# Two of four channel blocks of a depthwise convolution as products with diagonal matrices, and a jump over a loop that is announced

## The chip, the cores and the metric

The kernel runs on one core of a Trainium2 chip. The metric is the device time of one execution in microseconds, as the median of several runs. The engines are PE (TensorE, matrix products), DVE (VectorE), ACT (ScalarE), POOL (GpSimd) and SP (SyncE, whose queue starts the transfers here). Each engine works through its own row of instructions in order and waits on semaphores for the others.

## The reference

All values are float32. A first model (two layers of attention and feed-forward, left out here) gives `x`, 256 tokens of 1024 channels. A second one takes `x` and a context stream of 256 tokens through a mixer "AB" and a mixture of experts, then through a mixer "CD" and another mixture of experts on `x` alone. The change touches two places of it, the convolution of AB and the two mixtures:

```python
def _conv_module(u, conv_w, conv_b, ln_g, ln_b):
    a, gate = jnp.split(u, 2, axis=-1)
    glu = a * jax.nn.sigmoid(gate)
    y = lax.conv_general_dilated(glu, conv_w[:, None, :], window_strides=(1,),
                                 padding=[(CONV_WIDTH // 2, CONV_WIDTH // 2)],
                                 dimension_numbers=('NWC', 'WIO', 'NWC'),
                                 feature_group_count=B_WIDTH) + conv_b
    ...  # layer norm over the channels, then silu

def _mixer_ab(...):
    px = hx @ w_in
    ...
    ox = _dense_attn_blocks(_group(qx, A_KV_HEADS), jnp.concatenate([kc, kx], axis=2), jnp.concatenate([vc, vx], axis=2))
    bx = _conv_module(px[..., o_u:], conv_w, conv_b, ln_g, ln_b)
    yx = jnp.concatenate([_merge(ox), bx], axis=-1) @ w_out

# a mixture: each token goes to 2 of 32 experts
    hid = jax.nn.silu(xb @ w_gate[e]) * (xb @ w_up[e])
    return (hid @ w_down[e]) * wt[:, None]
```

The convolution has 31 taps and 512 channels, each channel on its own: `y[c, t] = sum over j of w[j, c] * glu[c, t + j - 15]`.

## The kernel before

**The convolution.** Channels lie on the partitions, in four blocks of 128; `GT` holds the gated input of a stream with 15 zeros at both ends, `y` (tile `cy`) the sum. For a stream `s` a tap is one instruction on DVE (L1310) over 128 channels and 256 tokens: `y = GT[shifted by j] * w[:, j] + y`; the tap 0 of a block is written by ACT with the bias. So a stream has four first taps on ACT and 120 taps on DVE. They aren't written in one go: `Spare` holds a queue of small pieces of work for an engine, and at each tick of the program (a step of the projections or of the attention of `beside`) an engine is given credit, its `share` of the tick, and takes pieces until the credit is used up. The numbers 0.85 (main stream) and 0.5 (context stream) are those shares. In this way the taps stand in DVE's row between the pieces of the main stream's attention.

**The attention beside it.** A step of the attention makes scores on PE (`acc<-KT,QT`, L1165), the maximum of each row on DVE (L1176, L1178), the exponentials on ACT (`P`, L1183), the transposes of `P` on PE (L788), their copy on ACT (L790) and the product with `V` on PE (L799). Before a head group PE transposes the queries (L1111), and ACT copies them (L1112). In between stand other products of PE (L319 to L321, three for each pair of tiles, with weights that ACT (L300) and DVE (L301) split in two parts). When all taps are done, the sums `cy` are turned by PE (L1339), and the layer norm over channels follows (L1345 to L1362), then the out projection.

**The experts.** `moe` runs over jobs of two experts each; in layer 0 a job "extra" stands at place 8. For a job PE makes gate and up products for the tokens (`project`, L1966, two halves `m` of 16 instructions, which leave 32 records each), ACT and DVE make `hd` of them (L1975, L1983), PE turns `hd` (`hidden_T`, L1989), and the down product follows (L2004). The result of the job before is added to the streams by `combine` for each of the token tiles: PE products with `PT` (L2013, L2065), DVE multiplies by the gate (`tm`, L2023), POOL adds (L2025). The tokens of a job are collected by `match` (DVE, `P`, L1932), `gather` (PE, L2136) and `turn_P` (PE). SP issues the transfers of the weights a fixed number of units ahead, each when a buffer comes free.

**The overflow loop.** Tokens that found no slot in their expert's place are counted in `over`. Behind the job at `i == OVER + 1` (8) all engines load that count (L2232), and if it is 0, as here, they jump over a loop that serves such tokens (L2233). All of the job's combines are written ahead of that jump.

Of the kernel before, what the change touches and what calls it, by code (L numbers as in the profile page):

```python
# [24 lines left out]
NE = 32  # L25
# [5 lines left out]
CONV = ((0.85, 0.1, 4), (0.5, 0.1, 4))  # L31
# [96 lines left out]
def body(tc, d, dump=None):  # L128
    nc = tc.nc
    es = ExitStack()  # L130
    with es:
# [1100 lines left out]
        class MixerAB:  # L1232
            CHUNKS = {"gate": (1280, 512), "a": (768, 512), "kv": (512, 256), "q": (0, 512)}

            def __init__(self, es):
                self.es = es
                wk = self.wk = es.enter_context(tc.tile_pool(name="ab", bufs=1, side="right"))

                for c0, n in ((C_CW, 124), (C_LG, 8)):
                    nc.vector.tensor_scalar(cols[:, c0:c0 + n], cols[:, c0:c0 + n], 0.5, None, op0=OP.mult)  # L1240
                self.tq, self.tk = rope_tables(wk, R_QA, True), rope_tables(wk, R_KA, False)
                self.QT = {1: wk.tile([128, 4, 256], F32, name="QTc")}
                self.KT = wk.tile([128, 512], F32, name="KT")
# [6 lines left out]
                self.spare = Spare(vector=0, gpsimd=0)  # L1250
                on_tick.append(self.beside)
# [52 lines left out]
            def tap(self, s, k, e, j):  # L1304
                w = cols[:, C_CW + 31 * k + j:C_CW + 31 * k + j + 1]
                v, g = self.y[s][:, k], self.GT[s][:, k, j:j + 256]
                if j == 0:
                    nc.scalar.activation(v, g, AF.Identity, scale=w, bias=col(C_CB + k))
                elif e == "vector":
                    nc.vector.scalar_tensor_tensor(v, g, w, v, op0=OP.mult, op1=OP.add)  # L1310
                else:
                    m = self.wk.tile([128, 256], F32, name="tap", bufs=4)
                    nc.scalar.activation(m, g, AF.Copy, scale=w)
                    nc.gpsimd.tensor_tensor(v, v, m, op=OP.add)

            def conv(self, s):
                dve, pool, n = CONV[s]
                self.spare.share = dict(vector=dve, gpsimd=pool)
                for e, ks in (("vector", range(n)), ("gpsimd", range(n, 4))):
                    for j in range(31):  # L1320
                        for k in ks:
                            self.spare.add(e, 0.1 if j == 0 else 0.4 if e == "vector" else 0.7,
                                           lambda k=k, j=j, e=e: self.tap(s, k, e, j))
                    self.spare.add(e, 0.0, lambda: self.half(s))
# [60 lines left out]
            def run(self, sp, norm, norms_done):  # L1385
# [526 lines left out]
        def moe(l, route, u0, during, ending, tail):  # L1912
# [3 lines left out]
            with ExitStack() as ph:  # L1916
# [4 lines left out]
                class Side:  # L1921
# [63 lines left out]
                    def hidden_T(self):  # L1985
# [4 lines left out]
                        self.hT = wr.tile([128, 4, 128], F32, name="hT")[:, :n]  # L1990
                        q3 = q[:, :n * 128].rearrange("p (k s) -> p k s", s=128)
                        nc.scalar.activation(self.hT, q3, AF.Copy)  # L1992
                        self.Y = [wr.tile([128, D], F32R, name="Yh"), wr.tile([128, D], F32R, name="Yl")]

                    def down(self, n, u):

                        if n == 0:
                            self.p = [acc(), acc()]
# [28 lines left out]
                class Half(Side):  # L2027
# [23 lines left out]
                    def down(self, n, u):  # L2051

                        if n == 0:
                            self.p = acc()
# [12 lines left out]
                class Last(Side):  # L2067
# [4 lines left out]
                    def down(self, n, u):  # L2072
                        p = acc()
# [19 lines left out]
                class Late(Half):  # L2093


                    def row(self, e, j, k):
# [14 lines left out]
                class Group:  # L2111


                    def __init__(self, sides, pool=wk):
                        self.sides, self.pool = sides, pool
                        self.n = 256 if pool is wk else 128 * len(sides)
# [22 lines left out]
                    def gather(self, tiles=order):  # L2139
                        XT = self.pool.tile([128, 8, self.n], F32, name="XT")  # L2140
# [27 lines left out]
                extra = []  # L2168
                prev = None
# [12 lines left out]
                for i, j in enumerate(jobs):  # L2182
                    cur = sides.pop(i)
                    if i % 2:

                        sides.update((n, side(jobs[n])) for n in range(i + 1, min(i + 3, len(jobs))))
                        group = Group(list(sides.values())) if sides else None
                        if group:
                            group.match()
                    nxt = sides.get(i + 1)  # L2190
                    for m in range(2):
# [24 lines left out]
                    for n in range(2):  # L2216
                        cur.down(n, u)
                        if nxt and n == 0:
                            nxt.weights()
# [7 lines left out]
                    if i == OVER + 1:  # L2227
                        for t4 in order:
                            prev.combine(t4)
                        prev = None  # L2230

                        total = nc.values_load(route.over[0:1, 0:1], min_val=0, max_val=NT * 4)  # L2232
                        with tc.If(total > 0, preferred_fallthrough_block=False), \  # L2233
                                tc.tile_pool(name=f"ov{l}", bufs=1) as ok:
                            at = ok.tile([128, 1], F32, name="at")
                            nc.vector.memset(at, float(EXTRA[l]))
                            with tc.For_i(0, total):
                                ei, sl, w1 = route.pick(ok, at)
                                e = nc.values_load(ei[0:1, 0:1], engines=(mybir.EngineType.SP,), min_val=0, max_val=NE - 1)
                                s = Late(sl, w1)  # L2240
                                late = Group([s], ok)
                                late.match()
                                late.gather()
                                s.turn_P()
                                s.weights()
                                for m in range(2):
                                    s.act(m, s.project(m, e))
                                s.hidden_T()
                                for n in range(2):
                                    s.down(n, e)  # L2250
                                for t4 in order:
                                    s.combine(t4)
                                nc.vector.tensor_scalar(at, at, 1.0, None, op0=OP.add)
# [289 lines left out]
```

## Time and profile before

| what | value |
| --- | --- |
| median of three runs | 2186.72 us (2186.63 to 2191.0) |
| profiled execution, its own time | 2184.34 us |
| its span | 2182.6 us |
| mean granted clock of PE | 0.964 |
| busy: PE, DVE, ACT, POOL | 91%, 48%, 34%, 18% |
| instructions | 28252 |

The span is what the profile sees of the execution, from the first instruction to the last; the device time has 1.7 us around it. The convolution of the main stream and its attention lie between 859 and 953 us, the experts of layer 0 between 1045 and 1560 us with the jump near 1308 us, those of layer 1 between 1735 and 2182 us with the jump near 1964 us. The shares are means over all stages, and no stage looks like the mean.

### The profile page before, as it was taken

What the parts mean: (1) busy time and instruction counts of PE and PEld (TensorE: products, weight loads), DVE (VectorE), ACT (ScalarE), POOL (GpSimd) and SP (SyncE); (2) the same over time, 40 slices, a digit from 0 to 9 for tenths busy, and PEclk for the clock granted to TensorE, in tenths of its full rate; (3) what the DMA queues carried; (4) which work ended last, traced back from release to release, by engine and by line L of the source; (5) the groups of instructions that cost most, each with busy time, mean ns of one, the idle gap of its engine ahead of it and who ended that gap; (6) DMA issues with size and microseconds to landing.
All of it is one profiled execution on the core that took longest, in us unless ns stands there. A gap on an engine that the chain in (4) does not pass through costs nothing. (4 is left out here: it accounts for less than half of the span.)

```text
span 2182.6 us, 28252 instructions
## 1 busy us (share of the span) xinstructions
PE 1986.8 (91%) x10991; PEld 1262.9 (58%) x10991; DVE 1037.2 (48%) x2123; ACT 734.8 (34%) x1287; POOL 399.3 (18%) x353
## 2 busy tenths in 40 slices
PE   8998999997999988667999998999788799998998
PEld 5765888774898767446444454444366444343343
DVE  5745554664658986957423332333553422222222
ACT  5544544555565456443111110111264311111110
POOL 3000110100110100015132342233420111121111
PEclk8999999999999999788999999999999899999999
DMA  9776777675565443105799997999552699999998
GB/s 324 279 259 211 242 247 267 212 270 176 171 204 174 155 146 115 39 20 203 319 420 414 412 410 295 411 417 417 202 212 78 267 421 421 420 421 383 421 421 340
DMA packets 160765, 612.98 MB, mean 281 GB/s; under 512 B 10528, under 2 KB 16256, under 8 KB 111345
## 3 DMA queue, kind: packets, MB, share of 16 engines
q1 hardware_dynamic: 155744, 596.86, 71.1%
q0 software_dynamic: 4448, 13.51, 2.2%
q8 instruction: 89, 1.46, 0.3%
q10 hardware_dynamic: 432, 0.74, 0.1%
q14 instruction: 52, 0.42, 0.1%
HBM read 607.90 MB, written 3.16 MB: 280 GB/s over the span
## 5 line engine op out<-in xcount | busy, mean ns | idle before, releaser
L1966 PE MATMUL acc<-w,XT 128*64 128x512 f32 x1856 | 435.8, 599 | 19.5 <-DVEq L2233 10.6
L301 DVE TENSOR_TENSOR w<-w 128x1024 fp32r<-128x1024 f32 x244 | 297.9, 1233 | 172.8 <-ACT w L300 154.9
L300 ACT ACTIVATE w<-w 128x1024 fp32r<-128x1024 f32 x252 | 264.5, 1059 | 193.9 <-PE acc L321 92.8
L1966 PEld LDWEIGHTS acc<-w,XT 128*64 128x64 f32 x1856 | 140.1, 138 | 280.8 <-issue 250.9
L2025 POOL TENSOR_TENSOR X<-X,tm 128x512 f32<-128x512 f32 x124 | 155.4, 1281 | 425.1 <-DVE tm L2023 425.1
L2023 DVE TENSOR_TENSOR tm<-acc,gate 128x512 f32<-128x512 f32 x196 | 129.7, 686 | 217.5 <-PE acc L2013 172.1
L2004 PE MATMUL acc<-w,hT 128*64 128x512 f32 x912 | 215.5, 598 | 6.0 <-ACT hT L1992 6.0
L363 PE MATMUL acc<-hi,w 128*128 128x256 f32 x576 | 163.9, 285 | 5.4 <-ACT hi L489 2.2
L364 PE MATMUL acc<-lo,w 128*128 128x256 f32 x576 | 161.9, 281 | 0.8 <-POOL lo L490 0.8
L365 PE MATMUL acc<-hi,w 128*128 128x256 f32 x576 | 161.8, 281 | 0.0
L321 PE MATMUL acc<-w,lo 128*128 128x512 f32 x368 | 150.0, 408 | 1.3 <-POOL lo L1378 1.2
L319 PE MATMUL acc<-w,hi 128*128 128x512 f32 x336 | 142.5, 424 | 6.7 <-ACT hi L1377 5.3
L320 PE MATMUL acc<-w,hi 128*128 128x512 f32 x336 | 137.1, 408 | 8.3 <-DVE w L301 8.2
L1992 ACT ACTIVATE hT<-trp 128x512 f32<-128x512 f32 (+1 forms) x33 | 19.5, 591 | 330.8 <-PE trp L1989 330.8
L1983 DVE SCALAR_TENSOR_TENSOR hd<-sg,ws,acc 128x512 f32<-128x512 f32 (+1 forms) x33 | 36.3, 1099 | 196.5 <-issue 101.0
L2025 POOL TENSOR_TENSOR C<-C,tm 128x512 f32<-128x512 f32 x64 | 79.5, 1272 | 273.8 <-DVE tm L2023 273.8
L2004 PEld LDWEIGHTS acc<-w,hT 128*64 128x64 f32 x912 | 63.4, 136 | 109.6 <-issue 97.4
L363 PEld LDWEIGHTS acc<-hi,w 128*128 128x128 f32 x576 | 108.7, 189 | 8.1 <-ACT hi L489 2.6
L2136 PE MATMUL acc<-P,hi 128*128 128x256 f32 x544 | 104.1, 289 | 8.9 <-issue 6.6
L365 PEld LDWEIGHTS acc<-hi,w 128*128 128x128 f32 x576 | 110.1, 191 | 0.0
L364 PEld LDWEIGHTS acc<-lo,w 128*128 128x128 f32 x576 | 109.1, 189 | 1.5 <-POOL lo L490 1.1
L417 ACT ACTIVATE Yh<-acc 128x512 fp32r<-128x512 f32 x63 | 37.6, 597 | 209.2 <-PE acc L2004 200.2
(423 smaller groups left out, 3427.8 us busy)
## 6 DMA issues: line engine op xcount, KB each, us to landing
w<-in_ex_gate_dram SPq DMA_DIRECT2D x118, 1024.0 KB, 13.2
w<-in_ex_up_dram SPq DMA_DIRECT2D x118, 1024.0 KB, 14.3
w<-in_ex_down_dram SPq DMA_DIRECT2D x118, 1024.0 KB, 13.0
w<-in_ffn_w_dram SPq DMA_DIRECT2D x64, 1024.0 KB, 5.3
fw<-in_mod_w_dram SPq DMA_DIRECT2D x48, 1024.0 KB, 7.5
w<-in_a_w_qkv_dram SPq DMA_DIRECT2D x17, 1024.0 KB, 10.0
w<-in_w_in_ab_dram SPq DMA_DIRECT2D x14, 1024.0 KB, 5.3
w<-in_b_w_qkv_dram SPq DMA_DIRECT2D x12, 1024.0 KB, 5.5
```

What stands on the lines that cost most here:

```text
L300: nc.scalar.activation(wh, w, AF.Copy)
L301: self.engine.tensor_tensor(wl, w, wh.bitcast(F32), op=OP.subtract)
L319: nc.tensor.matmul(ps[:, :n], xh, wh, start=first, stop=False)
L320: nc.tensor.matmul(ps[:, :n], xh, wl, start=False, stop=False)
L321: nc.tensor.matmul(ps[:, :n], xl, wh, start=False, stop=last)
L363: nc.tensor.matmul(z, wh[:, js], xh, start=k == 0 and j % 2 == 0, stop=False)
L364: nc.tensor.matmul(z, wh[:, js], xl, start=False, stop=False)
L365: nc.tensor.matmul(z, wl[:, js], xh, start=False, stop=k == 7 and j % 2 == 1)
L1966: nc.tensor.matmul(p[self.rows(a)], self.XT[:, 4 * k0 + k, self.rows(a)], units[v + a][:, k], start=k0 + k == 0, stop=4 * k0 + k == 7)
L2004: nc.tensor.matmul(self.p[c][self.rows(a)], self.hT[:, 2 * n + k, self.rows(a)], units[v + a][:, k, s], start=n + k == 0, stop=n + k == 2)
L2023: nc.vector.tensor_tensor(g, p, gates[s][:, c], op=OP.mult)
L2025: add.tensor_tensor(dst, dst, g, op=OP.add)
```

## The change

In the main stream's convolution (`CONV[0]`) the blocks 0 and 1 stay as taps on DVE. For the blocks 2 and 3 each tap becomes a product on PE: `sums += diag(w[:, j]) @ GT[shifted by j]`, 62 products that add up in one accumulator over the whole stage (L1341 of the new file, `acc<-GT,dg`), with 62 matrices `dg` that ACT makes by scaling the identity (L1332; four buffers, made three ahead of their use). Two ACT copies with the bias take the sums to `y` at the end. So 60 taps of DVE and two first taps of ACT go. The products are pieces of `Spare` for PE, at 0.43 of credit each and a share of 0.6, from the query projection on. The context stream is as before.

In both mixtures the count and the jump move from behind job `i == 8` into job 9, between `hidden_T` and the down product; the combines of job 8 are all written in the first half of job 9, `match` follows the jump, and `gather` and `turn_P` follow the first part of the down product. The loop's `If` gets a label, a hint for PE names it, and its body is now the block that follows the comparison directly; the block that is taken when nothing is left over stands behind it.

```diff
-CONV = ((0.85, 0.1, 4), (0.5, 0.1, 4))
+CONV = ((0.85, 2), (0.5, 4))
...
+                def weights(i):
+                    if i < len(todo):
+                        diag.append(self.wk.tile([128, 128], F32, name="dg", bufs=4))
+                        nc.scalar.activation(diag[i], ident, AF.Copy, scale=self.weight(*todo[i]))
+
+                def product(i):
+                    if i == 0:
+                        self.sums = acc().rearrange("p (k t) -> p k t", k=2)
+                        for a in range(3):
+                            weights(a)
+                    weights(i + 3)
+                    k, j = todo[i]
+                    nc.tensor.matmul(self.sums[:, k - n], diag[i], self.GT[s][:, k, j:j + 256], start=i == 0, stop=i == len(todo) - 1)
+
+                def end():
+                    for k in range(n, 4):
+                        nc.scalar.activation(self.y[s][:, k], self.sums[:, k - n], AF.Identity, bias=col(C_CB + k))
+                    self.half(s)
+
+                for i in range(len(todo)):
+                    self.spare.add("tensor", 0.43, lambda i=i: product(i))
+                self.spare.add("tensor", 0.0, end)
...
+                    self.spare.share["tensor"] = 0.6
...
+                def left_over():
+
+                    nonlocal ok
+                    total = nc.values_load(route.over[0:1, 0:1], min_val=0, max_val=NT * 4)
+                    with tc.If(total > 0, preferred_fallthrough_block=True, label=f"left{l}"), \
+                            tc.tile_pool(name=f"ov{l}", bufs=1) as ok:
...
+                    loop = i == OVER + 2
+                    if loop:
+                        tc.mark_branch_hint_location(f"left{l}", engines=[mybir.EngineType.PE])
...
-                            for t4 in order[m * half:(m + 1) * half]:
+                            for t4 in order if loop and m == 0 else () if loop else order[m * half:(m + 1) * half]:
                                 prev.combine(t4)
                     cur.hidden_T()
-                    if nxt:
+                    if loop:
+
+                        left_over()
+                        group = next_two()
+                        nxt = sides[i + 1]
+                    elif nxt:
...
-                    if i == OVER + 1:
-                        for t4 in order:
-                            prev.combine(t4)
-                        prev = None
-
-                        total = nc.values_load(route.over[0:1, 0:1], min_val=0, max_val=NT * 4)
-                        with tc.If(total > 0, preferred_fallthrough_block=False), \
-                                tc.tile_pool(name=f"ov{l}", bufs=1) as ok:
```

In PE's row of before, at the start of the main stream's attention (`qr`, `KT`, `QT`, `P`, `PT` and `V` are the queries, keys, probabilities and values), stand:

```order
L1111 MATMUL trp<-cst,qr 128x128 x4
L1165 MATMUL acc<-KT,QT 128x512 x4
L788 MATMUL trp<-cst,P 128x128 x8
L1165 MATMUL acc<-KT,QT 128x512 x2
L788 MATMUL trp<-cst,P 128x128 x4
L799 MATMUL acc<-PT,V 64x128 x8
L1111 MATMUL trp<-cst,qr 128x128 x4
```

In PE's row of the change the same place reads (L1341 is the product with a diagonal):

```order
L1341 MATMUL acc<-GT,dg 128x256 x6
L1111 MATMUL trp<-cst,qr 128x128 x4
L1165 MATMUL acc<-KT,QT 128x512 x2
L1341 MATMUL acc<-GT,dg 128x256 x4
L1165 MATMUL acc<-KT,QT 128x512 x2
L788 MATMUL trp<-cst,P 128x128 x4
L1341 MATMUL acc<-GT,dg 128x256 x4
L788 MATMUL trp<-cst,P 128x128 x4
L1165 MATMUL acc<-KT,QT 128x512 x2
L1341 MATMUL acc<-GT,dg 128x256 x5
L788 MATMUL trp<-cst,P 128x128 x4
L799 MATMUL acc<-PT,V 64x128 x8
```

Four more products and L1111 follow there; so 23 products stand ahead of the second L1111, in five groups, and 39 behind it, in twelve. The first four scores are parted: two, then products, then two. 

In ACT's row of the change, at the same place, stand (L1332 makes the diagonals; before, L1112 followed L300 directly, and between the exponentials stood only the copies of L790):

```order
L300 ACTIVATE w<-w 128x1024
L1332 ACTIVATE dg<-cst,cols 128x128 x9
L1112 ACTIVATE QT<-trp 128x4x128
L1183 ACT_TABLE_LOAD
L1183 ACTIVATE P,den<-acc,nm 128x512 x2
L1332 ACTIVATE dg<-cst,cols 128x128 x4
L1183 ACTIVATE P,den<-acc,nm 128x512 x2
L790 ACTIVATE PT<-trp 128x512
L1332 ACTIVATE dg<-cst,cols 128x128 x4
L790 ACTIVATE PT<-trp 128x512
L1183 ACTIVATE P,den<-acc,nm 128x512 x2
L1332 ACTIVATE dg<-cst,cols 128x128 x5
```

The first nine diagonals stand ahead of the exponentials, each further group behind a pair of them.

In PE's row of before, at the jump of layer 0, the last combines stand right ahead of the count:

```order
L2065 MATMUL acc<-Yl,PT 128x512
L2065 MATMUL acc<-Yh,PT 128x512
L2065 MATMUL acc<-Yl,PT 128x512
L2232 TENSOR_LOAD over
L2233 COMPARE_AND_BRANCH
L2233 UNCONDITIONAL_BRANCH
```

In PE's row of the change (L1993 is `project`, L2016 `hidden_T`, L2099 the combine of the extra job) it reads:

```order
L2099 MATMUL acc<-Yh,PT 128x512
L2099 MATMUL acc<-Yl,PT 128x512
L1993 MATMUL acc<-w,XT 64x512 x16
L2016 MATMUL trp<-cst,hd 128x128 x4
L2210 TENSOR_LOAD over
L2211 COMPARE_AND_BRANCH
```

A group of L1993 and the transposes of `hd` now stand between the last combine and the jump. The hint for this jump is the second row of PE's program (`L2591 BRANCH_PREFETCH_HINT`), and that for layer 1 stands behind the loop of layer 0.

## Rows read from the trace of the kernel before

**Rows 1.** Windows of 20 us: length, busy time (instructions) by engine, PEclk, DMA share, GB/s.

```profile
880.00:900.00 20.00, 7.72 (x24) 3.97 (x24) 18.51 (x46) 5.41 (x11) 0.00 (x0) 0.59 0.00 1
900.00:920.00 20.00, 16.36 (x90) 11.00 (x89) 19.61 (x47) 11.10 (x23) 0.00 (x0) 0.84 0.29 106
920.00:940.00 20.00, 19.10 (x140) 13.25 (x138) 17.88 (x44) 7.87 (x18) 1.89 (x2) 1.00 0.00 0
940.00:960.00 20.00, 9.56 (x65) 7.14 (x63) 12.35 (x37) 7.75 (x15) 0.66 (x1) 0.77 0.00 1
```

**Rows 2.** Timeline of DVE: start us, us, instruction, idle before and its releaser.

```profile
939.23 0.68 DVE L1176 TENSOR_REDUCE mx<-acc 128x1 f32<-128x512 f32 x1
...
940.80 4.83 DVE L1310 SCALAR_TENSOR_TENSOR cy<-GT,cols,cy 128x256 f32<-128x256 f32 x12
...
946.12 0.87 DVE L1310 SCALAR_TENSOR_TENSOR cy<-GT,cols,cy 128x256 f32<-128x256 f32 x2
```

**Rows 3.** Timeline of PE in the attention stage, columns as above.

```profile
880.53 1.09 PE L1111 MATMUL trp<-cst,qr 128*128 128x128 f32 x4 [4.43 <-DVE qr L1094]
886.36 3.44 PE L1165 MATMUL acc<-KT,QT 64*128 64x512 f32 x8 [4.74 <-ACT QT L1112]
...
898.71 2.08 PE L1165 MATMUL acc<-KT,QT 64*128 64x512 f32 x4
...
903.58 0.66 PE L1111 MATMUL trp<-cst,qr 128*128 128x128 f32 x4
...
910.16 0.79 PE L320 MATMUL acc<-w,hi 128*128 128x512 f32 x1 [2.60 <-DVE w L301]
...
918.23 0.63 PE L834 MATMUL trp<-cst,R 128*128 128x128 f32 x4 [0.68 <-DVE R L829]
...
936.55 0.66 PE L788 MATMUL trp<-cst,P 128*128 128x128 f32 x4 [0.90 <-ACT PT L790]
...
946.35 1.09 PE L834 MATMUL trp<-cst,R 128*128 128x128 f32 x4 [6.10 <-DVE R L829]
...
951.80 0.66 PE L1339 MATMUL trp<-cst,cy 128*128 128x128 f32 x4
```

**Rows 4.** Waits of PE from 1100 to 1300 us: total us, times, longest us.

```profile
PE acc L2004 <- ACT hT L1992: 0.9, 3, 0.3
```

**Rows 5.** Timeline of DVE at the jump of layer 0.

```profile
1313.60 0.69 DVE L2023 TENSOR_TENSOR tm<-acc,gate 128x512 f32<-128x512 f32 x1 [0.53 <-POOL X L2025]
```

**Rows 6.** Timeline of PE, L1966 in layer 0's loop over experts.

```profile
1252.87 7.04 PE L1966 MATMUL acc<-w,XT 128*64 128x512 f32 x32
...
1315.40 15.92 PE L1966 MATMUL acc<-w,XT 128*64 128x512 f32 x64 [7.92 <-DVEq L2233]
```

**Rows 7.** Waits of SP's queue from 1735 to 1960 us, the costliest.

```profile
SPq L227 <- DMA w<-in_ex_down_dram: 43.6, 21, 3.2
```

**Rows 8.** Timeline of PE, pool mixer of the last layer.

```profile
1623.62 0.60 PE L1570 MATMUL acc<-hi,U 128*128 128x256 f32 x2
...
1635.63 1.03 PE L1570 MATMUL acc<-hi,U 128*128 128x256 f32 x4
```

**Rows 9.** Timeline of ACT in the first block.

```profile
19.62 2.15 ACT L533 ACTIVATE hi<-trp,cols 128x128 fp32r<-128x128 f32 x8
```

**Rows 10.** Timeline of ACT in the attention stage.

```profile
884.78 1.04 ACT L300 ACTIVATE w<-w 128x1024 fp32r<-128x1024 f32 x1
...
894.68 1.28 ACT L1183 ACT_TABLE_LOAD   x1 [8.38 <-DVE nm L1178]
895.98 0.69 ACT L1183 ACTIVATE P<-acc,nm 128x512 f32<-128x512 f32 x1
```

**Rows 11.** The load of the count, layer 0: duration ns min/median/max, first and last start us.

```profile
L2232 PEldq EVENT_SEMAPHORE  x8: 51/51/51, 1306.8 to 1307.5; - x8
```

**Rows 12.** The jump's line in layer 0, columns as above.

```profile
L2233 PEldq COMPARE_BRANCH  x2: 98/2204/4309, 1308.2 to 1308.5; - x2
```

**Rows 13.** The jump's line in layer 1.

```profile
L2233 PEldq COMPARE_BRANCH  x2: 73/195/317, 1963.0 to 1964.2; - x2
```

More of the change, by code (lines that the diff above doesn't have):

```diff
@@ L1300, in q, with weight, tap @@
                     self.gone.add(s)
-            def tap(self, s, k, e, j):
-                w = cols[:, C_CW + 31 * k + j:C_CW + 31 * k + j + 1]
+            def weight(self, k, j):
+                return cols[:, C_CW + 31 * k + j:C_CW + 31 * k + j + 1]
+            def tap(self, s, k, j):
+                w = self.weight(k, j)
                 v, g = self.y[s][:, k], self.GT[s][:, k, j:j + 256]
@@ L1318, in conv @@
[L1318 to L1324, printed above, removed]
+                share, n = CONV[s]
@@ new lines, in conv @@
+                self.spare.share["vector"] = share
+                for j in range(31):
+                    for k in range(n):
+                        self.spare.add("vector", 0.1 if j == 0 else 0.4, lambda k=k, j=j: self.tap(s, k, j))
+                self.spare.add("vector", 0.0, lambda: self.half(s))
+                todo = [(k, j) for j in range(31) for k in range(n, 4)]
+                if not todo:
+                    self.half(s)
+                    return
+                diag = []
@@ L1326, in half @@
+                def end():
+                    for k in range(n, 4):
+                        nc.scalar.activation(self.y[s][:, k], self.sums[:, k - n], AF.Identity, bias=col(C_CB + k))
+                    self.half(s)
+                for i in range(len(todo)):
+                    self.spare.add("tensor", 0.43, lambda i=i: product(i))
+                self.spare.add("tensor", 0.0, end)
             def half(self, s):
@@ L1997, in down @@
                         if n == 0:
+                            self.new_Y()
                             self.p = [acc(), acc()]
@@ L2053, in down @@
                         if n == 0:
+                            self.new_Y()
                             self.p = acc()
@@ L2072, in down @@
                     def down(self, n, u):
+                        if n == 0:
+                            self.new_Y()
                         p = acc()
@@ L2093, in moe, with place @@
                 class Late(Half):
+                    def place(self):
+                        return ok
                     def row(self, e, j, k):
@@ L2168, in moe @@
                 extra = []
+                def left_over():
[3 more added lines that the diff above has]
+                            tc.tile_pool(name=f"ov{l}", bufs=1) as ok:
+                        at = ok.tile([128, 1], F32, name="at")
+                        nc.vector.memset(at, float(EXTRA[l]))
+                        with tc.For_i(0, total):
+                            ei, sl, w1 = route.pick(ok, at)
+                            e = nc.values_load(ei[0:1, 0:1], engines=(mybir.EngineType.SP,), min_val=0, max_val=NE - 1)
+                            s = Late(sl, w1)
+                            late = Group([s], 128)
+                            late.match()
+                            late.gather()
+                            s.turn_P()
+                            s.weights()
+                            for m in range(2):
+                                s.act(m, s.project(m, e))
+                            s.hidden_T()
+                            for n in range(2):
+                                s.down(n, e)
+                            for t4 in order:
+                                s.combine(t4)
+                            nc.vector.tensor_scalar(at, at, 1.0, None, op0=OP.add)
+                ok = None
                 prev = None
@@ L2189, in moe @@
                             group.match()
+                        return group
+                    if i % 2 and not loop:
+                        group = next_two()
                     nxt = sides.get(i + 1)
@@ L2208, in moe @@
                         if prev:
-                            for t4 in order[m * half:(m + 1) * half]:
+                            for t4 in order if loop and m == 0 else () if loop else order[m * half:(m + 1) * half]:
                                 prev.combine(t4)
                     cur.hidden_T()
-                    if nxt:
+                    if loop:
+                        left_over()
+                        group = next_two()
+                        nxt = sides[i + 1]
+                    elif nxt:
                         if i % 2:
@@ L2218, in moe @@
                         if nxt and n == 0:
+                            if loop:
+                                group.gather()
+                                nxt.turn_P()
                             nxt.weights()
@@ L2226, in moe @@
                     prev = cur
-                    if i == OVER + 1:
-                        for t4 in order:
-                            prev.combine(t4)
-                        prev = None
-                        total = nc.values_load(route.over[0:1, 0:1], min_val=0, max_val=NT * 4)
-                        with tc.If(total > 0, preferred_fallthrough_block=False), \
-                                tc.tile_pool(name=f"ov{l}", bufs=1) as ok:
[L2235 to L2253, printed above, removed]
                 tail(lambda t4: prev.combine(t4, (1,), nc.vector))
```

23 lines of the change are left out of this document (10 added, 13 removed).

## The prediction

> **What bounds the kernel now.** I read the windows first. From 880 to 940 us [rows 1] DVE is busy 18.5, 19.6 and 17.9 of each 20 us and DMA moves little, so no transfer sets the pace there and none can take up a delay. [...]
>
> The timeline of DVE shows where the conv ends [rows 2]: taps up to 946.99, one run of twelve from 940.80. PE's longest late idle, 6.10 us before the transposes of R at 946.35, is put down to DVE [rows 3], and the cy transposes start at 951.80. What follows is serial (layer norm, out projection, routing, experts), so a shift of 951.80 is a shift of everything behind it.
>
> Layer 0's loop over experts is bound by PE: from 1100 to 1300 us it waited 0.9 us on its costliest line [rows 4], so what the jump costs PE there is paid in full. At the jump DVE still worked through combines at POOL's pace up to 1314.3 [rows 5]; PE sat idle 7.92 us for it, and the 64 records of L1966 behind took 15.92 us, where 32 otherwise take 7.04 [rows 6]. That is 7.92 + 15.92 - 14.08 = **9.8 us** lost. In layer 1 SP's queue waits for transfers to land, 43.6 us on one line alone [rows 7]; there a stall of PE is not the bound.
>
> **Conv: what is added and removed.** A product is a 128x128 f32 weight against 128x256 f32. L1570 has this shape; its eight instructions leave 16 records, two for each. Two records in a row took 0.60 us and four 1.03 [rows 8], so each further one adds 0.215 us, and a product costs 0.43 us: 62 x 0.43 = **26.7 us of PE** at the full level, about 0.85 each at the lower. Removed are 60 taps of DVE, 0.40 us apart (4.83 us for twelve [rows 2]), 24 us. The 62 diagonals are ACT instructions of 128x128: eight of L533 took 2.15 us [rows 9], some 0.25 each with the last one's tail off, 15.5 us in all. ACT has that room on the whole (5.4, 11.1 and 7.9 of 20 us [rows 1]), but it works in order.
>
> **Conv, the floor.** PE's work in the stage, brought to the full level by the windows [rows 1], is 7.72 x 0.59 + 16.36 x 0.84 + 19.10 + 9.56 x 0.77 = 44.8 us; some 2.1 us of it, an estimate, lie behind 951.80, so 42.7. The first product can't run before ACT is through L300 at 885.8 [rows 10] and a diagonal of some 0.36: 886.2. With no idle from there, 42.7 + 26.7 = 69.4 us end at 955.6: **+3.8 us** against 951.80. Less needs cheaper products.
>
> **Conv, with its waits.** The rows of the program (section on the change) say how the queues stand; durations are those of rows 2, 3 and 10.
> Six products stand ahead of L1111, which began at 880.53. PE is idle until 886.2 and runs at the lower level behind that idle, as before (four transposes 1.09 us, against 0.66 at 903.58): 6 x 0.85 bring L1111 to 891.3, the copy of QT (some 0.6, an exp of that shape takes 0.69 [rows 10]) to 893.0, and the first pair of L1165 (half of 3.44) to 894.7. A pair's maxima take DVE 1.57 (939.23 to 940.80), the table load 1.28 beside the second, the two exps about 1.4 (0.69 each): done at 897.8. The tenth diagonal stands behind these exps on ACT, and the tenth product ahead of the second pair of scores on PE: PE waits to 898.2, and the second pair ends at 899.7, where it ended at 889.8 before. Maxima, exps and a copy bring the fourteenth diagonal to 903.6; then L788 and the third pair of scores, to 905.6 (900.8 before). Once more: the eighteenth product waits behind that pair's exps to 909.0, and behind it come another, L788, L799 and four products, so the second L1111 stands at about 913.2 instead of 903.58, **9.6 us later**.
> From there to 951.80 were 48.2 us, 10.3 of them idle (2.60, 0.68, 0.90 and 6.10 [rows 3]) and some 3.6 for the lower level (16.36 x 0.16 + 9.56 x 0.23, less what lies outside): 34.3 us of work. The other 39 products are 16.8 us: 51.1 us without a gap end at 964.3. Two copies with bias of about 0.6 us stand between the last product and the transposes, partly beside softmax transposes. I take **+13 us**; the upper bound, where each of the 12 groups left also waits a diagonal's 0.36 us, is +17.
>
> **The jump of layer 0.** The combines of job 8 now stand between two groups of L1966 and are done beside them, so DVE no longer holds the jump back. PE then pays its own way: eight waits and the load of the count, from 1306.8 to the first branch at 1308.2, 1.4 us [rows 11, 12]. What the branch over the body costs is open: 4.31 us in layer 0, where DVE's lateness hid it [rows 12], 0.32 in layer 1 [rows 13]. The body still lies between the branch and its target, and the hint that names it stands at the very start of PE's program, some 1300 us ahead. So I take the row of the same layer: 9.8 - 1.4 - 4.3 = **4.1 us** won. With the low row it is 8.1; with two more us at the lower level behind a stall of 5.7, 2.1.
> The row shows a jump over the body at 4.31 us. [...]
>
> **Layer 1.** PE's idle there is not on the path. SP still empties its queue of transfers at the jump, eight transfers later. I take 0, between 0.5 won and 0.5 lost. The tiles that change pools (hT, XT) belong to the loop that doesn't run.
>
> **Sum.** 13 - 4.1 + 0 = **+8.9 us**. On the profiled execution, 2184.34 us, that is 2193.2; on the median of the runs, 2186.72, which lies 2.4 above it, 2195.6. I forecast 2195.5.
>
> **Rivals**, on the median. (a) *Conv at its floor*: PE finds other work at each of the three waits above. For it: DVE has 24 us less to do; against it: the queues work in order, and the tenth diagonal stands behind the exps. 3.8 - 4.1 = 0: 2186.5, no change. (b) *The branch is cheap*, as in layer 1 or by the hint: 13 - 8.1 = +5, 2191.6. One row of two speaks for it, the row of the same layer against it. (c) *Each group waits for ACT*, with four buffers of diagonals and 15.5 us more among exps: 17 - 3 = +14, 2200.7. (d) *Faster: the product is cheap.* If the two records of a product overlap, it takes 0.215 us and PE's added work is 13.3 us: the conv comes out at 13 - 13.3 = 0 with the waits and at -9.6 at the floor, and the time is 2173 to 2183. It decides from 0.22 us a product down, or 0.36 without the waits, since the jump's 4 us are then left as a gain. The four records in 1.03 us speak against it.
>
> **Chances.** The forecast (conv +9 to +17, jump -2 to -5; 2190 to 2199 by itself) 0.48, (b) 0.20, (c) 0.10, (a) 0.13, (d) 0.09. A measurement of this kernel can tell about 0.2%, 4.4 us, from no change. Slower takes the forecast, (c) and six tenths of (b): 0.70; faster is (d) and a little of (a) with a cheap branch: 0.10; the same, 0.20. From 2184 (the floor with a branch of middling price) to 2202 leaves out 2 in 10.
>
> **What would show it.** Right: L1341 at 0.43 us a product, DVE under 16 of 20 us, PE without idle from some 913 to 964, the cy transposes near 965; in layer 0 PE's branch at about 4 us, with no idle put down to DVE there. Wrong: cy transposes before 957 (the waits are over-counted), products near 0.22 us, a branch under 1 us, or a gap behind the jump because transfers come late.

## The result, and the profile after

The change takes 2201.82 us (median of five runs, 2191.43 to 2202.91) against 2186.72, 15 us more; taken over all the runs, the ratio to before is **1.0057, with a 95% interval of 1.0039 to 1.0075**, or 12 us, slower. A second measurement on another occasion gave 2197.52 us and 1.0047 (1.0031 to 1.0063). The time forecast was 2195.5, the range 2184 to 2202; the median lies just inside its upper end. The profiled execution of the change took 2191.43 us, 7.1 more than that of before, and is the fastest of its runs; what follows explains these 7 us, and what the other runs have on top is a question of its own (below).

The windows of the attention stage after the change (columns as in [rows 1]):

```profile
880.00:900.00 20.00, 8.58 (x27) 5.92 (x27) 18.48 (x44) 8.12 (x19) 0.00 (x0) 0.66 0.00 0
900.00:920.00 20.00, 17.27 (x85) 11.04 (x86) 9.75 (x22) 13.11 (x32) 0.00 (x0) 0.91 0.00 0
920.00:940.00 20.00, 19.34 (x116) 14.65 (x115) 7.52 (x16) 10.88 (x29) 1.27 (x1) 1.00 0.30 106
940.00:960.00 20.00, 18.58 (x123) 13.60 (x121) 5.89 (x15) 13.16 (x36) 1.26 (x1) 1.00 0.00 1
```

DVE went from 18.5, 19.6 and 17.9 us to 18.5, 9.8 and 7.5; PE from 7.7, 16.4, 19.1 and 9.6 to 8.6, 17.3, 19.3 and 18.6. PE is now the engine of the stage.

The timeline of PE there, at the places of [rows 3]:

```profile
888.03 5.46 PE L1341 MATMUL acc<-GT,dg 128*128 128x256 f32 x12 [10.93 <-issue]
893.28 0.67 PE L1111 MATMUL trp<-cst,qr 128*128 128x128 f32 x4
894.64 1.13 PE L1165 MATMUL acc<-KT,QT 64*128 64x512 f32 x4 [0.69 <-ACT QT L1112]
...
899.97 0.99 PE L1341 MATMUL acc<-GT,dg 128*128 128x256 f32 x2 [2.71 <-ACT dg L1332]
...
906.37 0.70 PE L1341 MATMUL acc<-GT,dg 128*128 128x256 f32 x2 [1.17 <-ACT dg L1332]
...
911.61 1.13 PE L1341 MATMUL acc<-GT,dg 128*128 128x256 f32 x4 [1.56 <-ACT dg L1332]
...
914.14 2.00 PE L1341 MATMUL acc<-GT,dg 128*128 128x256 f32 x8
915.97 0.60 PE L1111 MATMUL trp<-cst,qr 128*128 128x128 f32 x4
...
924.47 1.56 PE L1341 MATMUL acc<-GT,dg 128*128 128x256 f32 x6 [0.66 <-ACT dg L1332]
...
957.51 1.13 PE L1341 MATMUL acc<-GT,dg 128*128 128x256 f32 x4 [1.42 <-ACT dg L1332]
...
969.77 0.98 PE L1365 MATMUL trp<-cst,cy 128*128 128x128 f32 x4
```

PE sits idle for 10.93 us up to 888.03, since six products (twelve records) now stand ahead of L1111 in its row. Its next long wait, 2.71 us at 899.97, is that of the tenth product for its diagonal behind the two exps, as forecast; the fourteenth (1.17 at 906.37) and the eighteenth (1.56 at 911.61) wait likewise. The second L1111 stands at 915.97 instead of 903.58, and the cy transposes at 969.77 instead of 951.80. Not all of these 18.0 us are the convolution's. DVE writes its input `GT` here, in before and then after the change:

```profile
857.67 1.28 DVE L1292 SCALAR_TENSOR_TENSOR GT<-cy,acc 128x512 f32<-128x512 f32 x2
```

```profile
859.85 1.28 DVE L1292 SCALAR_TENSOR_TENSOR GT<-cy,acc 128x512 f32<-128x512 f32 x2
```

So the trace of the change is 2.2 us late already at a place ahead of its edits. (Over the traces of all kernels here this input is written between 857.66 and 865.09 us, so traces differ by up to 7 us before any of the edits on the convolution or the jump comes into play.) From that point the transposes come 109.92 us later instead of 94.13: **+15.8 us**.

The products' line and that of the diagonals, by groups of instructions over the whole span (the columns are busy time and mean ns, then idle time before and its releasers):

```profile
L1341 PE MATMUL acc<-GT,dg 128*128 128x256 f32 x124 | 35.1, 422 | 18.4 <-issue 10.9 <-ACT dg L1332 7.5
...
L1332 ACT ACTIVATE dg<-cst,cols 128x128 f32<-128x128 f32 x62 | 21.7, 394 | 5.7 <-PE acc L1341 5.5
```

There are 124 records of products with 18.4 us of idle in front of them, 7.5 of it for diagonals.

The jump of layer 0 on PE, which answers to [rows 6]:

```profile
1330.19 7.09 PE L1993 MATMUL acc<-w,XT 128*64 128x512 f32 x32 [0.76 <-DVE tm L2056]
1338.60 0.66 PE L2016 MATMUL trp<-cst,hd 128*128 128x128 f32 x4 [1.31 <-DVE hd L2010]
1341.02 5.10 PE L2037 MATMUL acc<-w,hT 128*64 128x512 f32 x16 [1.76 <-ACTq L2211]
```

and PE's branch of the jump, in layer 0 first and then in layer 1 (duration in ns, then start), which answer to [rows 12, 13]:

```profile
L2211 PEldq COMPARE_BRANCH  x1: 393/393/393, 1340.0 to 1340.0; - x1
```

```profile
L2211 PEldq COMPARE_BRANCH  x1: 6068/6068/6068, 1990.4 to 1990.4; - x1
```

The 7.92 us in front of L1966 are gone. PE now waits 0.76 us for `tm` ahead of the second group of L1993, 1.31 us for `hd` ahead of the transposes, as it did before (1.30 at 1332.62), and 1.76 us behind them, put down to ACT's row, which is about the 1.4 us for the count [rows 11, 12] and the branch, 0.39 us instead of 4.31.

What this gave shows at work that both kernels have ahead of the jump and behind it, a group of transposes of `P` and a down product. In before, and then after the change:

```profile
1298.35 0.60 PE L1942 MATMUL trp<-cst,P 128*128 128x128 f32 x4
...
1345.04 3.65 PE L2004 MATMUL acc<-w,hT 128*64 128x512 f32 x16
```

```profile
1314.71 0.60 PE L1969 MATMUL trp<-cst,P 128*128 128x128 f32 x4
...
1354.57 3.65 PE L2037 MATMUL acc<-w,hT 128*64 128x512 f32 x16
```

The change is 16.4 us late ahead of the jump and 9.5 behind it: layer 0's jump gave **6.8 us** back. Another 2.4 us come back in the pool mixer between 1620 and 1660 us, but there the kernel with diagonals seven ahead (below), which has the jump of before, regains 2.1 us as well, so these are not shown to be the jump's. In layer 1 the branch took **6.07 us** where before it took 0.32. That makes the engines late there for a while, but DVE is 7.4 us late at 1900 us of before and 7.0 at 2050: layer 1 gave and cost as good as nothing, and the span ends 7.1 us late.

### The profile page after: what moved, and what is told of

The parts are those of the page before. It is cut to its first block, busy times and chain, and to the rows that moved or that the text cites. A ratio compares the mean times of both kernels' runs of the same rounds, so it can differ in the third digit from the quotient of the medians.

```text
span 2189.7 us, 28488 instructions
## 1 busy us (share of the span) xinstructions
PE 2012.7 (92%) x11115; PEld 1280.5 (58%) x11115; DVE 1012.2 (46%) x2063; ACT 755.4 (34%) x1349; POOL 398.4 (18%) x353
## 5 line engine op out<-in xcount | busy, mean ns | idle before, releaser
L1993 PE MATMUL acc<-w,XT 128*64 128x512 f32 x1856 | 432.6, 594 | 6.7 <-DMA w<-in_ex_gate_dram 4.5
L300 ACT ACTIVATE w<-w 128x1024 fp32r<-128x1024 f32 x252 | 264.5, 1059 | 192.2 <-PE acc L321 91.4
L1993 PEld LDWEIGHTS acc<-w,XT 128*64 128x64 f32 x1856 | 137.7, 137 | 268.3 <-issue 239.3
```

The source lines that it names most:

```text
L300: nc.scalar.activation(wh, w, AF.Copy)
L1993: nc.tensor.matmul(p[self.rows(a)], self.XT[:, 4 * k0 + k, self.rows(a)], units[v + a][:, k], start=k0 + k == 0, stop=4 * k0 + k == 7)
```

## The experiments

**Conv alone.** The convolution of the change, with the jump of before:

```diff
-CONV = ((0.85, 0.1, 4), (0.5, 0.1, 4))
+CONV = ((0.85, 2), (0.5, 4))
...
 (weights, product and end as in the change, nothing of the jump)
```

> The convolution of the change alone, with the jump of before. Theory (the products cost PE's work plus waits for diagonals): +15 us against before, the cy transposes 15 to 18 us later and everything behind them shifted by as much. Rival (the jump's gain is small and the conv costs less): +5 us or less. If the time of the change varies because of its jump, this kernel's runs lie as close together as those of before.

2209.93 us (2206.89 to 2212.48), ratio 1.0098 (1.0082 to 1.0115): 21 us slower. Its runs lie 5.6 us apart, those of before on that occasion 9.2. Its input is written at 861.78, 4.1 us late, and the transposes start at 971.96, 110.2 us later, 16.1 more than before. But then another 8.5 us are lost in the out projection: DVE's instructions are 19.0 us late at 974 us of before and 27.5 late at 990. PE's clock shows it; the windows of that stretch:

```profile
980.00:990.00 10.00, 4.81 (x15) 3.38 (x15) 0.80 (x2) 4.65 (x9) 1.28 (x1) 0.55 0.00 0
990.00:1000.00 10.00, 7.58 (x25) 5.50 (x25) 5.95 (x5) 5.12 (x8) 3.48 (x2) 0.79 0.13 32
1000.00:1010.00 10.00, 10.00 (x41) 9.22 (x41) 4.05 (x8) 5.32 (x11) 1.27 (x1) 0.50 0.70 221
1010.00:1020.00 10.00, 10.00 (x45) 8.21 (x44) 1.83 (x3) 1.52 (x4) 2.50 (x2) 0.85 1.04 371
```

PE's level falls to 0.50 with PE busy all the time. The timeline of PE, where it falls:

```profile
996.58 0.79 PE L321 MATMUL acc<-w,lo 128*128 128x512 f32 x1 [2.13 <-POOL lo L1404]
997.17 0.63 PE L319 MATMUL acc<-w,hi 128*128 128x512 f32 x1
```

PE waited 2.13 us for POOL's `lo`, and the products behind it lie 0.43 us apart instead of 0.23. In before the same wait is 1.21 us, and the level stays at 1.00 behind it:

```profile
976.64 0.50 PE L321 MATMUL acc<-w,lo 128*128 128x512 f32 x1 [1.21 <-POOL lo L1378]
```

So it does in the change's own profiled execution, where the wait is 1.25 us:

```profile
982.96 0.80 PE L319 MATMUL acc<-w,hi 128*128 128x512 f32 x1 [5.05 <-ACT hi L1403]
...
994.55 0.50 PE L321 MATMUL acc<-w,lo 128*128 128x512 f32 x1 [1.25 <-POOL lo L1404]
```

In that one the low level behind the 5.05 us of idle lasted longer (some 6.0 us from 982.96, against 3.9 from 985.16 in the convolution alone), so that PE came later to the point where it waits for POOL. The runs of the change that lie 10 us above its profile would fit an execution like that of the convolution alone; no trace shows one.

**Jump alone.** The jump of the change with the convolution of before (the hunks of the diff behind `CONV`).

> The jump of the change alone, with the convolution of before. Theory (PE's wait for the combines in layer 0 goes; the branch costs 0.4 us in some executions and 4 to 6 in others): between -9 us (cheap branch) and about 0 (dear branch), runs in two groups. Rival (the jump is worth -4 us always, and the spread comes from the convolution): -4 us with a spread of under 3 us.

2180.65 us (2175.32 to 2185.63), ratio 0.9967 (0.9953 to 0.9980): 7 us faster. PE's branch takes 0.398 us in layer 0 and 6.17 in layer 1, and at the two places of above the trace is 3.8 us late and then 1.9 early: 5.8 us from the jump of layer 0. The runs lie 10 us apart too, without two groups, and the one trace, of a run in their middle, has the cheap branch; both speak against the branch as what spreads them. The time of the convolution alone (+21 us) and this one (-7) add up to +14, between the two medians of the change (+15 and +10).

**The change once more**, unaltered.

> The change once more, unaltered, for a second trace: its timed runs lay 10 us apart (2191 and 2200 to 2203). If the branch is what differs, a slow execution shows PE's branch in layer 0 at over 4 us instead of 0.39, or one in layer 1 that the end pays for. If it is the convolution, the cy transposes lie at another time than 970.

2197.52 us (2191.51 to 2201.47), and its trace is once more of the fastest run (2191.51): branches 0.398 and 6.12 us, transposes 110.0 us behind the input, PE's wait for POOL 1.29 us. The branch and the convolution are the same from trace to trace. Neither trace is of a 2200 us run, so that those lose their time in the out projection is argued from the run of the convolution alone, not shown.

**One diagonal for all products.** The convolution alone, where ACT's 61 other diagonals are left out, and with them the weights of those taps:

```diff
+                        if i:
+                            diag.append(diag[0])
+                            return
+                        diag.append(self.wk.tile([128, 128], F32, name="dg", bufs=1))
```

> The convolution alone with a single diagonal that all 62 products use (the weights of the other taps are left out): the products stay, 61 instructions of ACT and PE's waits for them go. Theory of waits (product work fills idle time, most of the loss is waiting for diagonals and the later scores): +4 to +7 us against before. Rival (PE's work alone costs it): +13 us or more.

2197.92 us (2196.00 to 2202.85), ratio 1.0051 (1.0036 to 1.0067), +10 us by the medians: neither theory's number. The trace parts the two. The input is written at 861.35, and the transposes start here:

```profile
961.40 0.98 PE L1368 MATMUL trp<-cst,cy 128*128 128x128 f32 x4
```

That is 100.05 us, 5.9 more than before and 9.9 less than in the change. So the wait for diagonals and what follows from it is 10 us of the 15.8 (7.5 of it is the idle time in front of L1341 in the change), and PE's bare work 6. The rest is lost behind the convolution, again in the out projection, 3.4 us in this trace. There the wait for POOL is a little longer than in the change, and the level falls behind it, for a shorter time than in the convolution alone (PEclk 0.84 and 0.81 in the windows from 980 and 990):

```profile
986.18 0.50 PE L321 MATMUL acc<-w,lo 128*128 128x512 f32 x1 [1.45 <-POOL lo L1407]
```

**Diagonals earlier.** The convolution alone with eight buffers, seven ahead:

```diff
-                        diag.append(self.wk.tile([128, 128], F32, name="dg", bufs=4))
+                        diag.append(self.wk.tile([128, 128], F32, name="dg", bufs=8))
...
-                        for a in range(3):
+                        for a in range(7):
...
-                    weights(i + 3)
+                    weights(i + 7)
```

> The convolution alone with eight buffers of diagonals, made seven ahead instead of three. Theory (most of the loss is the products' wait for diagonals that stand behind exponentials on ACT, as the run with one diagonal says): the cy transposes come 7 to 10 us earlier than with three ahead, and the kernel is 5 to 10 us slower than before instead of 15 to 22. Rival (the 62 instructions on ACT cost as such, wherever they stand): no change against three ahead.

2196.81 us (2188.12 to 2202.83), ratio 1.0038 (1.0023 to 1.0053), +8 us, with all the arithmetic in place. The windows of the attention stage:

```profile
880.00:900.00 20.00, 12.29 (x50) 8.60 (x52) 18.52 (x46) 11.17 (x28) 0.00 (x0) 0.77 0.00 1
900.00:920.00 20.00, 20.00 (x120) 14.77 (x117) 12.66 (x27) 15.69 (x40) 0.00 (x0) 1.00 0.29 106
920.00:940.00 20.00, 20.00 (x121) 15.14 (x118) 4.68 (x12) 11.62 (x32) 1.27 (x1) 1.00 0.00 1
940.00:960.00 20.00, 19.96 (x145) 15.66 (x144) 4.16 (x9) 10.85 (x27) 1.26 (x1) 1.00 0.01 1
```

PE is busy all 20 of 20 us from 900 on. Its timeline at the two idle times left in the stage, at the transposes and at the wait for POOL:

```profile
891.55 1.13 PE L1165 MATMUL acc<-KT,QT 64*128 64x512 f32 x4 [0.69 <-ACT QT L1112]
...
896.84 0.65 PE L788 MATMUL trp<-cst,P 128*128 128x128 f32 x4 [1.18 <-ACT P L1183]
...
957.71 0.98 PE L1365 MATMUL trp<-cst,cy 128*128 128x128 f32 x4
...
982.29 0.80 PE L321 MATMUL acc<-w,lo 128*128 128x512 f32 x1 [2.12 <-POOL lo L1404]
```

957.71 is 100.05 us behind the input (857.66): the same +5.9 as with one diagonal. With seven ahead no wait for diagonals is left, and the 62 instructions cost nothing as such. The rival falls. PE's level falls here too behind 2.12 us for POOL, at 982.29 (PEclk 0.58 and 0.57 from 980 to 1000), and once more 8.5 us are lost.

**The hint.** The jump alone, without the two calls that place it:

```diff
-                    if loop:
-                        tc.mark_branch_hint_location(f"left{l}", engines=[mybir.EngineType.PE])
```

> The jump alone, new place and new layout of the blocks, without the two hints for PE. If the hint made layer 0's branch cheap (0.40 us), it now takes over 3 us and the kernel is 3 to 5 us slower than the jump alone; layer 1's branch stays near 6 us. If the hint does nothing, 0.40 and 6 us stay and the time is that of the jump alone, -7 us against before.

2184.52 us (2179.54 to 2189.39), ratio 0.9983 (0.9970 to 0.9996). PE's branch takes 0.357 us in layer 0 and 6.03 in layer 1: as with the hint. Its time lies some 4 us over the jump alone, on another occasion with runs 10 us apart. The branch does not explain it; the trace shows something else behind the cheap branch of layer 0:

```profile
1336.74 5.99 PE L2010 MATMUL acc<-w,hT 128*64 128x512 f32 x16 [6.89 <-DMA w<-in_ex_up_dram]
```

PE waits 6.89 us, put down to a transfer of weights, where the jump alone has 1.81: here the jump of layer 0 gives 1.1 us (7.0 late ahead of it, 5.9 behind). In the out projection this trace loses 3.5 us as well, behind a wait of 1.55 us for POOL. Whether the missing hint has to do with the late transfer, one trace can't show.

**The layout.** As the last, with the blocks of the `If` as before:

```diff
-                    with tc.If(total > 0, preferred_fallthrough_block=True, label=f"left{l}"), \
+                    with tc.If(total > 0, preferred_fallthrough_block=False), \
```

> The jump alone at its new place, no hint, and the blocks laid out as before (the comparison falls into the skip block, and a plain branch leads over the body). If the layout made layer 0's branch cheap, it takes some 4 us again, now in plain sight: -3 us against before instead of -7. If the place in the program decides, 0.4 us stay. In layer 1 the layout of before had 0.32 us.

2184.68 us (2179.73 to 2189.60), ratio 0.9983 (0.9970 to 0.9995). The prices of the branch have changed layers; in layer 0 (the two entries are the comparison and the branch over the body):

```profile
L2184 PEldq COMPARE_BRANCH  x2: 98/3034/5970, 1326.6 to 1326.9; - x2
```

The branch takes 5.97 us there, in plain view (PE idle 7.4 us, so that the jump gives 1.1 us here too), and 0.40 in layer 1. So the layout can decide; but with it all code behind the jump also stands elsewhere. The time is that of the kernel without the hint, in whose trace PE waited 6.89 us for a transfer at this place.

**The place of the code.** Tiny products of one column, whose sums nothing uses, ahead of layer 0's loop in the kernel before; 32 of them, then 64:

```diff
+                if l == 0:
+                    q = trp()
+                    for _ in range(32):
+                        nc.tensor.matmul(q[0:1, 0:1], ident[:, 0:1], ident[:, 0:1], start=True, stop=True)
```

> The kernel before with 32 tiny products (one column) ahead of layer 0's loop over experts, which move all later code of PE by 32 x 4 = 128 instructions and compute nothing that is used. If the price of the branch hangs on where code lies in the stream of instructions, the two layers change places: under 0.5 us for layer 0's branch instead of 4.3, and over 3 us for layer 1's instead of 0.32. If layer or traffic of the transfers decides, 4.3 and 0.32 stay.

> As the last, with 64 tiny products, 256 instructions. [...]

With 32 the two layers changed places. In layer 0 and then in layer 1:

```profile
L2237 PEldq COMPARE_BRANCH  x2: 98/204/309, 1312.2 to 1312.5; - x2
```

```profile
L2237 PEldq COMPARE_BRANCH  x2: 64/3013/5962, 1967.1 to 1968.4; - x2
```

With 64 they were as before again. In layer 0:

```profile
L2237 PEldq COMPARE_BRANCH  x2: 98/2208/4319, 1316.9 to 1317.3; - x2
```

with 0.317 in layer 1, as before to the nanosecond. 128 instructions let the two layers change places, 256 bring them back. With the jump of before, DVE is late at that place in any case [rows 5], and one run each, 2188.74 and 2194.18 us, says nothing of the time.

**One block instead of two**, diagonals seven ahead, jump of before:

```diff
-CONV = ((0.85, 2), (0.5, 4))
+CONV = ((0.85, 3), (0.5, 4))
```

> The convolution alone with one block of channels on the tensor engine instead of two (31 products, 30 taps of DVE gone), diagonals seven ahead. Theory (PE is the bound of the stage once 62 products lie in it; its idle time of some 16 us holds 13): between -3 and +3 us against before. Rival (any product in PE's row delays the scores): +8 us.

2176.35 us (2173.72 to 2177.61), ratio **0.9945** (0.9929 to 0.9960), 12 us faster: better than the theory, far off the rival. The timeline of PE where the stage ends:

```profile
934.31 0.78 PE L1365 MATMUL trp<-cst,cy 128*128 128x128 f32 x4
...
947.62 0.63 PE L1388 MATMUL trp<-cst,yt 128*128 128x128 f32 x4 [1.69 <-DVE yt L1379]
...
950.21 0.66 PE L834 MATMUL trp<-cst,R 128*128 128x128 f32 x4
```

The transposes come at 934.31, 71.0 us behind the input (863.30) instead of 94.1, ahead of the last head group, and the layer norm is done beside the rest of the attention. The transposes of R wait for nothing; now the attention ends last, and the convolution no longer does. The branch of the jump of before takes 0.309 us in layer 0 here and 6.06 in layer 1, as with the 32 tiny products: 31 products are 124 instructions.

**One block, three ahead.**

> One block on the tensor engine with the diagonals of the change (four buffers, three ahead), jump of before. Theory (products wait for diagonals behind exponentials with this order, as with two blocks): 5 to 10 us slower than with seven ahead, so -2 to -8 us against before. Rival (with one block PE's idle time takes these waits up): as with seven ahead, -12 us.

2182.27 us (2178.59 to 2186.47), ratio 0.9965 (0.9953 to 0.9978): 7 us faster than before, 5 less than with seven ahead. The transposes come 78.0 us behind the input. The order of the diagonals costs 7 us with 31 products, against 10 with 62.

**One block and the jump.**

> One block on the tensor engine with diagonals seven ahead, and the jump of the change with its hint. If both gains add: -12 and -7, -19 us against before. [...]

2170.26 us (2165.80 to 2178.12), ratio **0.9914** (0.9891 to 0.9937), 19 us faster than before, the fastest kernel here. Layer 0's branch took the high price. 31 products are 124 of PE's instructions, 124 fewer than the 62 of the change, and the two layers have changed places, as they did with 128 in the run with 32 tiny products:

```profile
L2211 PEldq COMPARE_BRANCH  x1: 6040/6040/6040, 1314.6 to 1314.6; - x1
```

with 0.381 us in layer 1. The trace agrees with the dear branch: it is 9.1 us early ahead of the jump and 9.9 behind it, so that the jump of layer 0 gives 0.9 us. The time is at the full sum all the same, 6 us beyond the 12 of one block and this 0.9; where the rest comes from stays open, and the interval, 14 to 24 us faster, is five us each way.

## Why the prediction was right, step by step

**PE is the bound of the stage: right.** With one diagonal and with diagonals seven ahead PE works 60 us with next to no gap (busy 59.7 and 60.0 us from 900 to 960), and in both the transposes come 5.9 us later than before. That is the floor, put at +3.8. It was 2 us low: it has no idle time from the first product on, and with seven ahead PE still waits 0.69 us for `QT` and 1.18 for `P`, which is about as much.

**The waits: right in place, a little small.** The tenth, fourteenth and eighteenth product waited where the rows said. The second L1111 came 12.4 us later than in [rows 3], 10.2 with the late start of that trace taken off (9.6 forecast), and the transposes 15.8 (13 forecast). What was left out are PE's waits for diagonals in later groups, 0.66 us at 924.47 and 1.42 at 957.51, which the forecast had put to the upper bound (+17). ACT's diagonals took 21.7 us, 0.35 each, where the prediction had 0.25 and 15.5; its +13 doesn't rest on that.

**Price of a product: right.** Eight records in a row took 2.00 us (914.14) and six 1.56 (924.47), so a further one adds 0.22 and a product costs 0.44 us, where 0.43 was forecast. The 0.85 us of a product at the lower level had no row; the six products at 888.03, with PEclk at 0.50 throughout, took 5.46 us, 0.91 each. Rival (d), a product at 0.215, is out.

**The jump of layer 0: right in kind, mis-sized.** Forecast 4.1 us won, measured 6.8 us in the trace of the change, 5.8 in that of the jump alone and 7 in its time. The term that was off is the branch: "I take the row of the same layer" (4.31 us) was the wrong row, 0.39 is what layer 0 got, and a branch under 1 us was one of the prediction's own signs of being wrong. Rival (b) has this number, but for a reason that it didn't name: not the layer and not the hint. Its 8.1 us are a little more than came, since PE's level was low for a while behind the idle (PEclk 0.70 from 1341 to 1346): the 16 records of the down product took 5.10 us at 1341.02, and 3.65 at 1354.57. The price belongs to the place of the code in PE's stream of instructions, as the runs with 32 and 64 tiny products show: 128 instructions turn the two layers round (0.309 us in layer 0 and 5.962 in layer 1), 256 leave them as they were (4.319 and 0.317). What PE does in the 4.0 to 6.2 us of a dear branch was not shown. The 62 products of the change are 248 instructions (124 matmul records and 124 weight loads of L1341), eight fewer than the 256 of the 64 tiny products, and layer 0's branch stayed as in the jump alone (0.39 us, 0.40 there); with the jump of before its price stayed at 4.0 to 5.0 us. 31 products are 124, and the prices changed layers (0.309 and 6.062 us with the jump of before). Of layer 1's 6 us nothing showed in the time, as forecast.

**The time: near, and in part by luck.** In the profile the sum is 2.2 us ahead of the convolution, +15.8 in it, 1.6 made good on the way to the jump, 6.8 won there and some 2.4 behind it: +7.1. Of the forecast's two terms, 13 - 4.1 = +8.9, the runs gave 15.8 - 6.8 = +9.0: a loss that was 2.8 us larger and a gain that was 2.7 us larger cancel. The median is +15 (12 by all the runs, 10 on the second occasion), and what it has above +9 no step of the prediction names. "A shift of 951.80 is a shift of everything behind it" leaves out PE's clock in the out projection, where the convolution alone lost 8.5 us more in its trace; that the change's slower runs lost theirs there is not shown. Rival (c), 2200.7, is nearer to the first median than the forecast, and the forecast nearer to the second, 2197.52; but of (c)'s terms the jump at -3 is not what the traces show, and only two of the twelve later groups wait for ACT.

**Faster or not.** The rival (a), the convolution at its floor, is what the kernel with seven ahead does in the stage (+5.9); with the jump of before it is still slower, by that and by the clock behind it. Seven ahead with two blocks and the new jump was not run. That one block would be 12 us faster was not in the prediction's eye: it costed the 62 as a whole and not the point where PE's idle time ends.

## What to carry to other kernels

Work moved to an engine with idle time paid up to that idle time and no further here: 31 products gained 7 to 12 us and 62 lost 8 to 21, up to 8.5 of that by the clock behind them. When a helper feeds it in order behind other work (diagonals on ACT behind exps), make the helper's output far enough ahead, else the bound engine waits in its own row (10 of the 15.8 us here). And when a branch over much code is priced, look at where the code stands, not at the layer: 128 instructions ahead of it changed its price from 0.32 us to 5.96 in layer 1 and from 4.31 to 0.31 in layer 0, so measure it where it will stand.

## What the runs showed of the hardware that was not expected

PE's branch over the loop cost 0.3 to 0.4 us in one layer and 4.0 to 6.2 in the other, in every kernel here (4.31 in layer 0 and 0.32 in layer 1 before, 0.39 and 6.07 in the change), and 128 instructions more in front let them change places (0.31 and 5.96) while 256 brought them back (4.32 and 0.32). A hint for the branch placed at the start of PE's program or some 650 us ahead changed neither price (0.398 and 6.17 us with, 0.357 and 6.03 without).

In the out projection PE's granted clock stayed high behind a wait for POOL of 1.12 to 1.29 us (PEclk 1.00 behind it in before, both traces of the change and the jump alone). It fell, with PE busy, behind waits of 1.45 and 1.55 us in the same place (PEclk 0.84 and 0.81, 0.82 and 0.83 in the two windows of 10 us from 980), which cost 3.4 and 3.5 us, and for longer behind 2.12 (0.58 and 0.57) and 2.13 (0.79, 0.50 and 0.85 in three windows from 990), which cost 8.5. The wait was the longer in these traces the earlier the level had risen ahead of it: some 6.4 us of low level behind the 5.05 us of idle and a wait of 1.12 us in the jump alone, 3.9 and 2.13 in the convolution alone. Whether that is what sets runs of one kernel some 10 us apart stays open, as does what the up to 7 us by which traces differ ahead of the convolution have to do with it.
